# Feeding a state-space scan: inputs in SBUF, four f32 row groups, and no stacking through DRAM

## The chip, the core and the metric

The kernel runs on one core of a Trainium2 chip. Its time is the device time of one execution in microseconds: 2395.61 us is the median of three runs (2390.84 to 2396.46). Everything is computed in one launch.

## What is computed

One layer of a hybrid decoder on 304 token columns: 16 meta tokens, 256 prompt tokens and 8 x 4 sample tokens. Around the mixer stand two SwiGLU blocks; the change lies inside the mixer, in the S5 branch.

```python
z = rms(x) @ w_in                      # u_pool | u_ssm | gate a | gate b
a_out = pool_mix(u_pool)
# S5, 64 groups of 16 channels, 64 complex states each
lam_bar = exp(lam * exp(log_dt));  b_bar = (lam_bar - 1) / lam * b
bu = einsum('blgc,gpc->blgp', u, b_bar)
bu[:, 0] += lam_bar * h0               # each sequence starts from its own state
h[t] = lam_bar * h[t-1] + bu[t]
y = real(einsum('blgp,gcp->blgc', h, c)) + d * u
s = gelu(y);  s = s * sigmoid(s @ glu_w + glu_b)
x = x + (sig(gate_a) * (a_out @ w_a) + sig(gate_b) * (s @ w_b)) @ w_out
```

## The kernel before

Channels lie on partitions and tokens on columns, so a product with a weight matrix streams 304 columns (288 once the meta tokens are dropped). Each weight chunk (512 x 256, 512 KB) is split on the chip into a high part `whi` (ScalarE, L143) and a rest `wlo` (VectorE, L152); `mm3` (L241) makes three one-pass matmuls of each product. `proj` (L427) takes one chunk after another and calls `step` (L211) after each: the high part of a later chunk, the functions left by the last projection (`g.post`), the low part, the next load on SyncE's queue, and then pieces of a side program, `g.rate` pieces per step on average. A fraction is carried over, and `g.owed` may start below zero, which delays the side program by `LAG` steps. Three raw buffers and four of each part bound how far the loads run ahead.

In the mixer the side program is first the pool branch, and from the second `u_ssm` projection on the scan (`Scan.run`, L900). Its order is written out in `run`: for each of 16 blocks of 2 x 128 states twelve pieces (`rows`, L863), which are mostly one VectorE instruction each. The recurrence is turned into a real one by multiplying with tables of cosines and sines `ee`, which the setup (a side program in FFN 1) has computed and left in DRAM. Two `tensor_tensor_scan` instructions (L867) per block run along the 2 x 304 columns with the decay `d0`, which is zero where a sequence starts.

The scan's inputs are made as follows. `u_in` (L1026) multiplies the projection by the norm's factor, splits u into a high and a low part, writes u to DRAM on SyncE's queue (`usc`), and writes high, low and high again to DRAM on GpSimd's queue in the layout `stk[4, 96, 304]`. `load` (L816) fetches for each block 96 rows of that into one of two SBUF tiles, whose last 32 rows are ones at the columns where a sample sequence starts (`isc`), then `bl`, the matrices of the block, `ee`, and every second time u. `into` (L829) makes one one-pass matmul of 128 rows for each of three kinds (real, imaginary, sum) and two halves; ScalarE copies each result to a tile `bu`. The matrix holds the high part of the input map twice, its rest once, and the start states in its last rows, so that the start states enter in the same product.

`outof` (L838) multiplies the states by the output map `clhs`: for each of eight channel tiles twelve f32 matmuls with 32 columns of weights, which write four groups of 32 rows of one bank. `act` (L849) adds d * u and applies GELU.

PSUM has eight banks of 512 f32: four for projections, three (`psaux`) for small products, one (`pslong`) for the output group and for part of the down projections.

Of the kernel before, what the change touches and what calls it, by code (L numbers as in the profile page):

```python
# [18 lines left out]
P = 128  # L19
# [6 lines left out]
NB = 8  # L26
# [10 lines left out]
MIXRATE = 2.35  # L37
# [10 lines left out]
LAG = 7  # L48
BUFS = 6
KUFS = 8  # L50
# [6 lines left out]
def host_consts():  # L57
    import numpy as np

    c = np.zeros((P, NT + NTV + 2), np.float32)  # L60
    c[:, :NT] = 1.0
    c[:, 0] = 0.0
    c[:, S0:NT:NS] = 0.0
    c[:, NT:NT + 16] = np.arange(16)
    c[:, NT + 16:NT + NTV] = 16 * np.arange(NA)
    par = (np.arange(P) // 16) % 2
    c[:, NT + NTV] = par == 0
    c[:, NT + NTV + 1] = par == 1
    s = np.zeros((32, NT), np.float32)
    for b in range(NB):  # L70
        s[b, S0 + b * NS] = s[NB + b, S0 + b * NS] = 1.0
    return {"consts": c, "starts": s}
# [90 lines left out]
def setup(ctx, tc, I):  # L163
# [21 lines left out]
    g.isc = g.dram.tile([32, JB, NT], F32R, name="isc")  # L185
# [352 lines left out]
def ssm_setup(g):  # L538
# [6 lines left out]
    g.clhs = [C.tile([P, NJ, 32], F32, name=f"clhs{i}") for i in range(3)]  # L545
    g.esc = [g.dram.tile([P, 3, JB, NT], F32, name=f"esc{b}") for b in range(NJ // JB)]
    g.bsc = [g.dram.tile([P, 3 * JB, P], F32R, name=f"bsc{b}") for b in range(NJ // JB)]
    tv = g.hc[:, NT:NT + NTV]

    with ExitStack() as cs_:  # L550
# [163 lines left out]
        ah = [T(f"ah{i}", [P, NB, NJ]) for i in range(3)]  # L714
# [7 lines left out]
        tt(ah[2], ah[0], ah[1], ALU.add)  # L722
# [18 lines left out]
        ind = T("q1", [32, NT])  # L741
        nc.gpsimd.dma_start(ind, I["starts"])
        yield 1
        cx = [T(f"cx{i}", [P, 8, 2, 64]) for i in range(3)]
        for i in range(3):
            for a in range(2):
                ts_(cx[i][:, :, a], cs[i], g.hc[:, NT + NTV + a:NT + NTV + a + 1], None, ALU.mult)
                yield 1

        G = 4  # L750
        bds = {}

        def spread(h, i):
            if i == 0:
                bds[h] = T("bd", [P, G, 3, P], bufs=2)
                nc.gpsimd.memset(bds[h], 0.0)  # L756
            hj = slice(h * G, (h + 1) * G)
            bv = bds[h][:, :, i, :96].rearrange("p j (r a c) -> p j r a c", r=3, a=2)
            for a in range(2):
                for r in range(3):  # L760
                    nc.scalar.copy(bv[a * 64:(a + 1) * 64, :, r, a], bx[i][a * 64:(a + 1) * 64, hj])
            for r in range(2):
                nc.scalar.copy(bds[h][:, :, i, 96 + r * NB:96 + (r + 1) * NB], ah[i][:, :, hj].rearrange("p b j -> p j b"))

        def turned(h, q, jj, bl):
            ps = bank(g, "bt", aux=True)
            for i in range(3):
                nc.tensor.transpose(ps[:, i * P:(i + 1) * P], bds[h][:, q * JB + jj, i], g.ident)
# [4 lines left out]
        indr = sp.tile([32, JB, NT], F32R, name="indr")  # L773
        for h in range(NJ // G + 1):
            if h == NJ // G:
                for jj in range(JB):
                    nc.vector.tensor_copy(indr[:, jj], ind)
                nc.gpsimd.dma_start(g.isc, indr)
                yield 1
            if h < NJ // G:  # L780
                for i in range(3):
                    spread(h, i)
                    yield 1
            if h >= 1:
                for q in range(G // JB):
                    bl = sp.tile([P, 3 * JB, P], F32R, name=nm(g, "bl"), tag="bl", bufs=2)
                    for jj in range(JB):
                        turned(h - 1, q, jj, bl)
                        yield 1
                    nc.gpsimd.dma_start(g.bsc[(h - 1) * (G // JB) + q], bl)  # L790
        for i in range(3):
            for q in range(2):
                ps = bank(g, "ct", aux=True)
                for ii in range(4):
                    nc.tensor.transpose(ps[:, ii * P:(ii + 1) * P], cx[i][:, q * 4 + ii].rearrange("p a s -> p (a s)"), g.ident)
                nc.scalar.activation(g.clhs[i][:, q * 16:(q + 1) * 16].rearrange("p j c -> p (j c)"), ps,
                                     AF.Copy, scale=-1.0 if i == 1 else 1.0)
                yield 1


class Scan:


    def __init__(self, g, sp, usc, stk):
        self.g, self.sp, self.usc, self.up = g, sp, usc, stk
        self.st = g.mix.tile([P, 2, NB + 1, NJ], F32, name="states")
        self.stk = [sp.tile([P, JB, NT], F32R, name=f"stk{i}") for i in range(2)]
        for t in self.stk:
            g.nc.gpsimd.dma_start(t[96:], g.isc)
        self.sparts = []  # L810
        self.yps = {}
# [3 lines left out]

    def load(self, sb):  # L816
        g, sp, nc = self.g, self.sp, self.g.nc
        i, half = divmod(sb, 4 // JB)
        ee = sp.tile([P, 3, JB, NT], F32, tag="ee", name=nm(g, "ee"), bufs=2)
        bl = sp.tile([P, 3 * JB, P], F32R, tag="bl", name=nm(g, "bl"), bufs=1)  # L820
        nc.gpsimd.dma_start(self.stk[sb % 2][:96], self.up[i][half * JB:(half + 1) * JB].rearrange("j r t -> r j t"))
# [508 lines left out]
```

## Time and profile before

| | |
|---|---|
| median of three runs | 2395.61 us |
| profiled execution | 2394.65 us |
| its span, first to last instruction | 2392.9 us |
| TensorE busy | 2351.8 us, 98% |
| VectorE busy | 1592.3 us, 67% |
| ScalarE busy | 1013.1 us, 42% |
| GpSimd busy | 137.9 us, 6% |
| DMA | 443.27 MB, 185 GB/s |

Shares are means over the span; what an edit is worth is read in the stretch where it lies. PE is TensorE's matmuls, PEld its weight loads, DVE is VectorE, ACT ScalarE, POOL GpSimd, SP SyncE; an engine's name with a q is its queue. Matmuls overlap, and the duration of one is longer than the distance to the next, so distances between starts or counts per stretch are used for what one costs. An f32 matmul is two records, a one-pass matmul is one.

### The profile page before, as it was taken

Reading aid. Unit: us, or ns where it says so; the run is one execution under the profiler, and the core shown is the slowest. Engines: PE = TensorE matmul, PEld = TensorE weight load, DVE = VectorE, ACT = ScalarE, POOL = GpSimd, SP = SyncE. Lnnn points to the kernel's source line nnn. Section 1 sums busy time; section 2 is a strip of 40 time slices with the busy share of each in tenths; the row PEclk is TensorE's granted clock in tenths of the full one; section 3 lists DMA queues with packets and bytes.
Section 4 is the critical chain, followed back from the end, with each engine's and each line's share of the span. In section 5 each row is a group of like instructions: output and inputs, shape, how many; then the busy total and the mean of one; then the engine's idle time right before and its main releaser. Section 6 shows DMA issues by size and latency. Waiting matters only on the chain.

```text
span 2392.9 us, 42570 instructions
## 1 busy us (share of the span) xinstructions
PE 2351.8 (98%) x17321; PEld 2333.2 (98%) x17321; DVE 1592.3 (67%) x2416; ACT 1013.1 (42%) x1617; POOL 137.9 (6%) x233
## 2 busy tenths in 40 slices
PE   8999999999999999979999999999999999999998
PEld 7999999999999999979989999999999999999997
DVE  6788777776555557659889875555555555555555
ACT  5333333343564335434545544443333333333334
POOL 1000000001010002220101031000000000000000
PEclk9999999999999999989999999999999999999999
DMA  6555666666556446697778676455555555555553
GB/s 187 159 159 187 192 199 205 206 197 184 180 175 191 154 156 196 183 256 230 241 232 251 197 253 206 151 177 167 164 163 168 167 168 166 166 163 167 168 167 111
DMA packets 407076, 443.27 MB, mean 185 GB/s; under 512 B 25036, under 2 KB 393904, under 8 KB 406872
## 3 DMA queue, kind: packets, MB, share of 16 engines
q1 hardware_dynamic: 376512, 376.75, 50.5%
q0 software_dynamic: 30368, 63.80, 9.1%
q8 instruction: 136, 2.23, 0.4%
q14 instruction: 60, 0.49, 0.1%
HBM read 404.30 MB, written 36.51 MB: 184 GB/s over the span
## 4 chain that ended last, share of the span: by engine, by line
PE 81%; issue 7%; DVE 5%; DMA 5%; ACT 2%; POOL 1%; ACTq 0%; SPq 0%; DVEq 0%; POOLq 0%
PE pj L243 20%; PE pj L244 19%; PE pj L245 19%; PE dn L243 7%; PE dn L245 7%; PE dn L244 7%; DMA raw<-in_w_in 2%; DVE wlo L152 2%; ACT whi L143 1%; DMA raw<-in_w_branch_a 1%; DMA bl<-bsc 1%; DMA raw<-in_ffn_w_gate 1%; DVE bu L867 0%; POOL bd L756 0%; PE tx L415 0%
## 5 line engine op out<-in xcount | busy, mean ns | idle before, releaser
L152 DVE TENSOR_TENSOR wlo<-raw,whi 128x1024 fp32r<-128x1024 f32 x698 | 852.6, 1223 | 592.2 <-ACT whi L143 587.0
L143 ACT CAST whi<-raw 128x1024 fp32r<-128x1024 f32 x698 | 732.5, 1051 | 1116.9 <-PE pj L244 611.3
L243 PE MATMUL pj<-X,whi 128*128 128x304 f32 (+1 forms) x2432 | 739.1, 304 | 0.0
L244 PE MATMUL pj<-X,whi 128*128 128x304 f32 (+1 forms) x2432 | 733.1, 301 | 0.0
L245 PE MATMUL pj<-X,wlo 128*128 128x304 f32 (+1 forms) x2432 | 732.0, 301 | 0.0
L243 PE MATMUL pj<-Y,whi 128*128 128x288 f32 x1728 | 509.8, 295 | 0.7 <-DVE Y L272 0.7
L244 PE MATMUL pj<-Y,whi 128*128 128x288 f32 x1728 | 510.1, 295 | 0.0
L245 PE MATMUL pj<-Y,wlo 128*128 128x288 f32 x1728 | 508.7, 294 | 0.0
L243 PEld LDWEIGHTS pj<-X,whi 128*128 128x128 f32 x2432 | 459.6, 189 | 3.5 <-issue 2.8
L244 PEld LDWEIGHTS pj<-X,whi 128*128 128x128 f32 x2432 | 460.8, 189 | 0.0
L245 PEld LDWEIGHTS pj<-X,wlo 128*128 128x128 f32 x2432 | 460.4, 189 | 0.0
L243 PEld LDWEIGHTS pj<-Y,whi 128*128 128x128 f32 x1728 | 325.3, 188 | 1.4 <-DVE Y L272 0.9
L244 PEld LDWEIGHTS pj<-Y,whi 128*128 128x128 f32 x1728 | 324.8, 188 | 0.0
L245 PEld LDWEIGHTS pj<-Y,wlo 128*128 128x128 f32 x1728 | 324.7, 188 | 0.0
L243 PE MATMUL dn<-H,whi 128*128 128x304 f32 x704 | 213.6, 303 | 0.2 <-DVE x L481 0.2
L245 PE MATMUL dn<-H,wlo 128*128 128x304 f32 x704 | 213.0, 303 | 0.0
L244 PE MATMUL dn<-H,whi 128*128 128x304 f32 x704 | 212.2, 301 | 0.0
L244 PE MATMUL dn<-X,whi 128*128 128x288 f32 x704 | 207.9, 295 | 0.0
L243 PE MATMUL dn<-X,whi 128*128 128x288 f32 x704 | 207.8, 295 | 0.0
L245 PE MATMUL dn<-X,wlo 128*128 128x288 f32 x704 | 207.6, 295 | 0.0
L243 PEld LDWEIGHTS dn<-H,whi 128*128 128x128 f32 x704 | 132.3, 188 | 0.5 <-DVE x L481 0.5
L243 PEld LDWEIGHTS dn<-X,whi 128*128 128x128 f32 x704 | 132.7, 188 | 0.0
(274 smaller groups left out, 1981.7 us busy)
## 6 DMA issues: line engine op xcount, KB each, us to landing
raw<-in_ffn_w_gate SPq DMA_DIRECT2D x176, 512.0 KB, 3.6
raw<-in_ffn_w_up SPq DMA_DIRECT2D x176, 512.0 KB, 3.6
raw<-in_ffn_w_down SPq DMA_DIRECT2D x176, 512.0 KB, 3.5
raw<-in_w_in SPq DMA_DIRECT2D x96, 512.0 KB, 5.2
raw<-in_w_out SPq DMA_DIRECT2D x32, 512.0 KB, 4.2
esc<-ee POOLq DMA_DIRECT2D x16, 912.0 KB, 5.0
ee<-esc POOLq DMA_DIRECT2D x16, 912.0 KB, 8.0
raw<-in_w_branch_a SPq DMA_DIRECT2D x16, 512.0 KB, 4.7
```

What stands on the lines that cost most here:

```text
L143: self.g.nc.scalar.copy(hi, self.raw[i])
L152: self.g.nc.vector.tensor_tensor(lo, raw, hi.bitcast(F32), ALU.subtract)
L243: mm(ps, wh, x[0], start=start, stop=False)
L244: mm(ps, wh, x[1], start=False, stop=False)
L245: mm(ps, wl, x[0], start=False, stop=stop)
```

## The change

The stacked tiles, the copies of u in DRAM and the row of ones go. `Scan.input` keeps u of each of eight channel tiles in SBUF as f32. For one tile and one kind `into` makes four f32 matmuls of 32 rows each, from partitions 0, 32, 64 and 96 of u and of the matrices, into four banks: three of `psaux` and `pslong`. Four copies on ScalarE bring them to the tiles of both blocks of the channel tile. The start states are no longer in the product: `begun` adds them on VectorE, two small additions per block. The setup makes one matrix tile `bc` per channel tile, input and output map together, and `matrices` loads it. The scan runs in place (`k3` and `k2`), all rows come from one ring of 15 tiles, the first loads are issued after the second pool projection, and the side program's rate is 2.25 instead of 2.35 with a lag of 2 instead of 7.

```diff
-MIXRATE = 2.35
+MIXRATE = 2.25
-LAG = 7
-BUFS = 6
-KUFS = 8
+LAG = 2
+ROWS = 15
...
-    g.clhs = [C.tile([P, NJ, 32], F32, name=f"clhs{i}") for i in range(3)]
+    g.ah = C.tile([P, 2, NB, NJ], F32, name="ah")
...
-    g.bsc = [g.dram.tile([P, 3 * JB, P], F32R, name=f"bsc{b}") for b in range(NJ // JB)]
+    g.bsc = [g.dram.tile([P, 2, 3, P], F32, name=f"bsc{i}") for i in range(KW)]
...
-            b3 = bl[:, jj * 3:jj * 3 + 3].rearrange("p i s -> p (i s)")
-            nc.scalar.copy(b3, ps[:, :3 * P])
-            tt(b3[64:96 + NB], ps[64:96 + NB, :3 * P], b3[64:96 + NB].bitcast(F32), ALU.subtract)
+            nc.scalar.copy(bc[:, half].rearrange("p i s -> p (i s)"), ps[:, :3 * P])
...
+    def input(self, ps, r):
+
+        u = self.sp.tile([P, NT], F32, name=nm(self.g, "u"))
+        self.g.nc.vector.tensor_tensor(u, ps, r, ALU.mult)
+        self.u.append(u)
+
     def load(self, sb):
...
-        nc.gpsimd.dma_start(self.stk[sb % 2][:96], self.up[i][half * JB:(half + 1) * JB].rearrange("j r t -> r j t"))
-        nc.gpsimd.dma_start(bl, g.bsc[sb])
-        nc.gpsimd.dma_start(ee, g.esc[sb])
...
+        g.nc.gpsimd.dma_start(ee, g.esc[sb])
+        return dict(ee=ee, bu={})
+
+    def matrices(self, i):
+        g = self.g
+        self.mats[i] = self.sp.tile([P, 2, 3, P], F32, tag="bc", name=nm(g, "bc"), bufs=2)
+        g.nc.gpsimd.dma_start(self.mats[i], g.bsc[i])
+
+    def into(self, i, pair, ri):
+
+        g = self.g
+        pss = []
+        for q in range(4):
+            rows = slice(q * 32, (q + 1) * 32)
+            ps = bank(g, "bu", aux=True, pool=g.pslong if q == 3 else None)[:, :NT]
+            g.nc.tensor.matmul(ps, self.mats[i][rows, 0, ri], self.u[i][rows], start=True, stop=True)
+            pss.append(ps)
+        for s in pair:
+            s["bu"][ri] = self.tile("row", ROWS)
+        for q, ps in enumerate(pss):
+            g.nc.scalar.copy(pair[q // JB]["bu"][ri][:, q % JB], ps)
...
+        def begun(k, ri):
+            tt(k[:, :, S0::NS], k[:, :, S0::NS], g.ah[:, ri, :, js].rearrange("p b j -> p j b"), ALU.add)
...
-                lambda: tt(k3, k1, k3, ALU.subtract),
-                lambda: scan(gr, d0, k3),
+                lambda: turned(k3, k1, k3, 0),
+                lambda: scan(k3, d0, k3),
...
+    def first(self):
+
+        self.matrices(0)
+        self.nxt = self.load(0)
+
     def run(self):
...
+        pair = [self.nxt, self.load(1)]
+        for ri in (2, 1, 0):
+            self.into(0, pair, ri)
+            yield 1
+        done, acts = None, None
+        for i in range(KW):
+            nxt = [dict(bu={}) for _ in range(half)]
+            for h in range(half):
+                sb = i * half + h
+                rows = self.rows(sb, pair[h])
+                if sb >= 1 and sb + 1 < nb:
+                    new = self.load(sb + 1)
+                    (nxt[0] if h else pair[1])["ee"] = new["ee"]
+                for n, row in enumerate(rows):
+                    row()
+                    if h == 0 and n == 3 and done is not None:
+                        self.outof(i - 1, done)
+                        acts = self.act(i - 1)
+                    if h == 0 and n == 8 and i + 1 < KW:
+                        self.matrices(i + 1)
+                    if h and i + 1 < KW and n in (4, 7, 10):
+                        self.into(i + 1, nxt, {4: 2, 7: 1, 10: 0}[n])
+                    yield 1
...
-    def u_in(i, ps):
-        u = Z()
-        nc.vector.tensor_tensor(u, ps, norm.r, ALU.mult)
-        hi, lo = uparts[i % 2]
-        nc.scalar.copy(hi, u)
-        nc.vector.tensor_tensor(lo, u, hi.bitcast(F32), ALU.subtract)
-        uk = g.dram.tile([P, NL], F32, name=nm(g, "usc"))
-        nc.sync.dma_start(uk, u[:, NMETA:])
-        stk = g.dram.tile([4, 96, NT], F32R, name=nm(g, "stk"))
-        for k, x in enumerate((hi, lo, hi)):
-            nc.gpsimd.dma_start(stk[:, k * 32:(k + 1) * 32], x)
...
+                if p == 1:
+                    scan.first()
...
+                g.post += [lambda q=q: scan.input(q, norm.r) for q in ps]
```

On TensorE, at the scan's first products, before: two `bu` products behind the ninth weight chunk after the first u projection, three behind the tenth, one behind the eleventh; `pj` are the matmuls of the projection.

```order
L245 MATMUL pj_11573<-X_10133,wlo_11501 128x304
L835 MATMUL bu_11625<-stk_10586,bl_11566 128x304
L835 MATMUL bu_11628<-stk_10586,bl_11566 128x304
L243 MATMUL pj_11572<-X_10180,whi_11529 128x304
...
L245 MATMUL pj_11573<-X_10232,wlo_11531 128x304
L835 MATMUL bu_11662<-stk_10586,bl_11566 128x304
L835 MATMUL bu_11665<-stk_10586,bl_11566 128x304
L835 MATMUL bu_11669<-stk_10586,bl_11566 128x304
...
L245 MATMUL pj_11573<-X_10330,wlo_11561 128x304
L835 MATMUL bu_11702<-stk_10586,bl_11566 128x304
```

The scan's first products on TensorE now, behind the third weight chunk after the first u projection: each four `bu` are one kind, one for each row group.

```order
L240 MATMUL pj_10937<-X_9989,wlo_10924 128x304
L812 MATMUL bu_11034<-u_10964,bc_10441 128x304
L812 MATMUL bu_11036<-u_10964,bc_10441 128x304
L812 MATMUL bu_11038<-u_10964,bc_10441 128x304
L812 MATMUL bu_11040<-u_10964,bc_10441 128x304
L812 MATMUL bu_11048<-u_10964,bc_10441 128x304
L812 MATMUL bu_11050<-u_10964,bc_10441 128x304
L812 MATMUL bu_11052<-u_10964,bc_10441 128x304
L812 MATMUL bu_11054<-u_10964,bc_10441 128x304
L238 MATMUL pj_10936<-X_10035,whi_10962 128x304
```

The first products moved six chunks, 144 projection matmuls, up in TensorE's order, and two groups of four stand back to back.

On GpSimd's queue, before, at the start of the scan: twelve writes of the stacks of four tiles, and behind them the scan's first loads.

```order
L1036 DMA stk_11457<-Y_10597 4x32x304
L1036 DMA stk_11467<-Y_10599 4x32x304
L1036 DMA stk_11467<-Y_10600 4x32x304
L1036 DMA stk_11467<-Y_10599 4x32x304
L821 DMA stk_10586<-stk_11315 96x2x304
L822 DMA bl_11566<-bsc_715 128x768
L823 DMA ee_11565<-esc_699 128x1824
L826 DMA u_11570<-usc_11313 128x288
```

The same queue now: the first matrices and tables stand among the pool branch's small transfers, two projections further up.

```order
L1010 DMA out<-up_10399 8x4x256
L803 DMA bc_10441<-bsc_712 128x768
L797 DMA ee_10443<-esc_696 128x1824
L960 DMA hist_10445<-in_state_pool 120x256
...
L1010 DMA out<-up_10888 8x4x256
L797 DMA ee_11032<-esc_697 128x1824
L803 DMA bc_11249<-bsc_713 128x768
L797 DMA ee_11327<-esc_698 128x1824
```

What the queue carries for a channel tile is now two `ee` and one `bc`; the stack writes, the stack reads, the second `bl` and u are gone.

On VectorE, one block of the scan now (before, the same rows without L864, and with the scans' results in other tiles):

```order
L872 TENSOR_TENSOR row_11110<-row_11109,row_11110 128x608
L864 TENSOR_TENSOR row_11110<-row_11110,ah 128x2x8
L849 SCALAR_TENSOR_TENSOR row_11110<-d_1665_11106,row_11110 128x608
L879 TENSOR_TENSOR row_11111<-row_11100,ee_10443 128x608
L872 TENSOR_TENSOR row_11111<-row_11109,row_11111 128x608
L864 TENSOR_TENSOR row_11111<-row_11111,ah 128x2x8
L849 SCALAR_TENSOR_TENSOR row_11111<-d_1665_11106,row_11111 128x608
```

Between each difference and its scan stands one addition of 2 x 8 columns more.

## Rows read from the trace of the kernel before

**Rows 1.** Page, engine totals: busy us, share of the span, instructions.

```profile
PE 2351.8 (98%) x17321; PEld 2333.2 (98%) x17321; DVE 1592.3 (67%) x2416; ACT 1013.1 (42%) x1617; POOL 137.9 (6%) x233
```

**Rows 2.** Stretches: from:to, length, busy us (instructions) by engine, clock, DMA share.

```profile
960.00:1020.00 60.00, 60.00 (x432) 59.96 (x432) 38.71 (x77) 22.93 (x38) 14.32 (x23) 1.00 0.65 176
...
1020.00:1080.00 60.00, 45.74 (x301) 45.06 (x301) 35.72 (x49) 25.78 (x45) 13.64 (x21) 0.86 0.98 259
...
1600.00:1800.00 200.00, 200.00 (x1514) 200.00 (x1513) 110.98 (x148) 74.72 (x87) 0.00 (x0) 1.00 0.53 166
```

**Rows 3.** The same table, stretches of 10 us.

```profile
1020.00:1030.00 10.00, 4.19 (x30) 3.94 (x29) 0.03 (x1) 1.04 (x1) 0.54 (x1) 0.83 1.15 286
1030.00:1040.00 10.00, 6.00 (x24) 6.04 (x25) 5.28 (x7) 3.61 (x6) 4.80 (x7) 0.50 0.86 227
```

**Rows 4.** Timeline: start, us, engine, line, what, count [idle before <- releaser].

```profile
1028.89 1.04 ACT L143 CAST whi<-raw 128x1024 fp32r<-128x1024 f32 x1 [12.78 <-DMA raw<-in_w_in]
...
1033.99 0.59 PE L835 MATMUL bu<-stk,bl 128*128 128x304 f32 x1 [9.80 <-DMA bl<-bsc]
```

**Rows 5.** DMA issues, 1017 to 1345 us: count, KB each, median us to landing.

```profile
raw<-in_w_in SPq DMA_DIRECT2D x65, 512.0 KB, 5.8
...
ee<-esc POOLq DMA_DIRECT2D x16, 912.0 KB, 8.0
...
bl<-bsc POOLq DMA_DIRECT2D x16, 384.0 KB, 4.4
...
stk<-stk POOLq DMA_DIRECT2D x16, 228.0 KB, 9.0
...
stk<-Y POOLq DMA_DIRECT2D x12, 152.0 KB, 10.2
```

**Rows 6.** Timeline, first matmul of the stage behind the scan.

```profile
1355.62 0.29 PE L243 MATMUL pj<-Y,whi 128*128 128x288 f32 x1
```

**Rows 7.** Lines, 1017 to 1345 us: count | busy us, mean ns | idle before.

```profile
L152 DVE TENSOR_TENSOR wlo<-raw,whi 128x1024 fp32r<-128x1024 f32 x84 | 102.4, 1219 | 41.6 <-ACT whi L143 41.3
...
L867 DVE TENSOR_TENSOR_SCAN bu<-d,kk 128x608 f32<-128x608 f32 x32 | 45.5, 1422 | 0.7
...
L836 ACT COPY bu<-bu 128x304 f32<-128x304 f32 x96 | 35.8, 411 | 31.7 <-PE bu L835 31.7
...
L889 DVE TENSOR_TENSOR kk<-kk,kk 128x608 f32<-128x608 f32 x16 | 12.6, 790 | 0.3
...
L1042 DVE TENSOR_TENSOR z<-pj,rs_y 128x288 f32<-128x288 f32 x28 | 11.4, 449 | 0.0
...
L895 DVE TENSOR_TENSOR kk<-bu,ee 128x576 f32<-128x576 f32 x15 | 11.3, 751 | 0.0
...
L835 PE MATMUL bu<-stk,bl 128*128 128x304 f32 x96 | 25.1, 325 | 17.5 <-DMA bl<-bsc 9.8 <-ACT bu L836 7.7
...
L884 DVE TENSOR_TENSOR states<-kk,kk 128x18 f32<-128x18 f32 x30 | 4.4, 192 | 0.4
...
L853 DVE SCALAR_TENSOR_TENSOR gy<-u,vec,yps 128x288 f32<-128x288 f32 x7 | 3.5, 500 | 0.0
```

**Rows 8.** Chain that ended last: start us, us, what.

```profile
1053.94 8.56 DMA raw<-in_w_branch_a
```

**Rows 9.** Timeline of TensorE around one output group.

```profile
1247.44 0.30 PE L244 MATMUL pj<-X,whi 128*128 128x288 f32 x1
1247.57 0.29 PE L245 MATMUL pj<-X,wlo 128*128 128x288 f32 x1
1247.79 1.66 PE L846 MATMUL yps<-kk,clhs 128*32 128x288 f32 x24
1249.39 0.40 PE L243 MATMUL pj<-X,whi 128*128 128x288 f32 x1
1249.62 0.29 PE L244 MATMUL pj<-X,whi 128*128 128x288 f32 x1
```

**Rows 10.** Timeline, f32 matmuls with two columns each.

```profile
940.28 0.72 PE L343 MATMUL ss<-ones,acc 128*128 128x2 f32 x6
```

More of the change, by code (lines that the diff above doesn't have):

```diff
@@ L68, in host_consts @@
     c[:, NT + NTV + 1] = par == 1
[L69 to L72, printed above, removed]
+    return {"consts": c}
 class Ctx:
@@ L713, in ssm_setup @@
         t8 = T("q1", [P, NB, NJ])
-        ah = [T(f"ah{i}", [P, NB, NJ]) for i in range(3)]
+        ah = [g.ah[:, i] for i in range(2)]
         tt(ah[0], h0[0], bc(lbr), ALU.mult)
@@ L721, in ssm_setup @@
         tt(ah[1], ah[1], t8, ALU.add)
-        tt(ah[2], ah[0], ah[1], ALU.add)
         yield 1
@@ L765, in turned, with spread @@
-        def turned(h, q, jj, bl):
+        bds = [T(f"bd{k}", [P, 3, 4, 2, 16]) for k in range(2)]
+        for bd in bds:
+            nc.gpsimd.memset(bd, 0.0)
+            yield 1
+        def spread(m):
+            for i in range(3):
+                for a in range(2):
+                    rows = slice(a * 64, (a + 1) * 64)
+                    nc.scalar.copy(bds[m % 2][rows, i, :, a], bx[i][rows, m * 4:(m + 1) * 4])
+        def turned(bc, half, src):
             ps = bank(g, "bt", aux=True)
@@ L791, in ssm_setup @@
[L791 to L798, printed above, removed]
+                nc.tensor.transpose(ps[:, i * P:(i + 1) * P], src(i), g.ident)
@@ L801, with __init__ @@
 class Scan:
-    def __init__(self, g, sp, usc, stk):
-        self.g, self.sp, self.usc, self.up = g, sp, usc, stk
+    def __init__(self, g, sp):
+        self.g, self.sp = g, sp
         self.st = g.mix.tile([P, 2, NB + 1, NJ], F32, name="states")
-        self.stk = [sp.tile([P, JB, NT], F32R, name=f"stk{i}") for i in range(2)]
-        for t in self.stk:
-            g.nc.gpsimd.dma_start(t[96:], g.isc)
+        self.u = []
         self.sparts = []
-        self.yps = {}
+        self.mats, self.yps = {}, {}
@@ L876, in rows @@
             nc.scalar.activation(d0[:, jj], g.hc[:, :NT], AF.Copy, scale=g.rdec[:, j:j + 1])
-        k1, k3, k2 = (self.tile("kk", KUFS) for _ in range(3))
+        k1, k3, k2 = (self.tile("row", ROWS) for _ in range(3))
         s["k"] = (k1, k2, k3)
-        gr, gi = bi, br
         js = slice(sb * JB, (sb + 1) * JB)
+        def begun(k, ri):
+            tt(k[:, :, S0::NS], k[:, :, S0::NS], g.ah[:, ri, :, js].rearrange("p b j -> p j b"), ALU.add)
         def states():
@@ L898, in rows @@
+                lambda: tt(L(k1), L(k1), L(er), ALU.mult),
                 states]
+    def first(self):
+        self.matrices(0)
+        self.nxt = self.load(0)
     def run(self):
+        half = 4 // JB
         nb = NJ // JB
-        nxt = self.load(0)
-        yield 1
-        yield 1
-        for k in range(6):
-            self.into(0, nxt, k)
-            yield 1
-        pair, acts = [], None
-        for sb in range(nb):
-            cur = nxt
-            rows = self.rows(sb, cur)
-            nxt = self.load(sb + 1) if sb + 1 < nb else None
-            for n, row in enumerate(rows):
-                row()
-                if nxt is not None and 6 <= n < 12:
-                    self.into(sb + 1, nxt, n - 6)
-                if len(pair) == 4 // JB and n == 3:
-                    i = (sb - 1) // (4 // JB)
-                    self.outof(i, pair)
-                    acts = self.act(i, pair[0]["u"])
-                    pair = []
-                yield 1
-                if acts is not None and n >= 6 and next(acts, None) is None:
-                    acts = None
-            pair.append(cur)
@@ L926, in run @@
-        self.outof(KW - 1, pair)
-        yield 1
-        yield from self.act(KW - 1, pair[0]["u"])
+        pair = [self.nxt, self.load(1)]
+        for ri in (2, 1, 0):
+            self.into(0, pair, ri)
+            yield 1
+        done, acts = None, None
[16 more added lines that the diff above has]
+                        self.into(i + 1, nxt, {4: 2, 7: 1, 10: 0}[n])
+                    yield 1
+                    if acts is not None and n >= 6 and next(acts, None) is None:
+                        acts = None
+            done, pair = pair, nxt
@@ L930, in store @@
+        self.outof(KW - 1, done)
+        yield 1
+        yield from self.act(KW - 1)
     def store(self, O, sp):
@@ L1049, in mixer @@
             sp = cs.enter_context(g.tc.tile_pool(name="scan", bufs=1))
-            scan = Scan(g, sp, usc, stks)
+            scan = Scan(g, sp)
             pool = Pool(g, O)
-            uparts = [(part(g, "Y", NT), part(g, "Y", NT)) for _ in range(2)]
             dparts, aparts = [], []
```

90 lines of the change are left out of this document (27 added, 63 removed).

## Prediction

> **What bounds the kernel now.** I read the page's engine totals first: TensorE is busy for 98% of the span [rows 1], so an edit can only pay where TensorE stands idle, runs slowly, or gets more or less to do. Next I read the table of stretches. At full pace TensorE issues 432 matmuls of 304 columns in 60 us, 0.139 us each, and of 288 columns 1514 in 200 us, 0.132 us each [rows 2]. The stretch from 1020 to 1080 us has only 301, and its granted clock is 0.86 [rows 2]. That is the start of the scan, which the change rewrites. The finer table shows 30 matmuls from 1020 to 1030 us and 24 from 1030 to 1040, at a granted clock of 0.83 and 0.50 [rows 3].
>
> The timeline says why. TensorE waits 9.80 us, until 1033.99, for the scan's first matrices `bl` to land, and ScalarE waits 12.78 us for a weight chunk at the same time [rows 4]. The DMA share is 1.15 from 1020 to 1030 [rows 3]. What is in flight there is the stacking: `stk<-Y` takes 10.2 us to land, `stk<-stk` 9.0 us, for 152 and 228 KB, while a 512 KB weight chunk takes 5.8 us [rows 5]. After its idle time TensorE runs at the lower of its two clocks (1.2 of 2.4 GHz: the 0.50 of rows 3) before it is back at full speed.
>
> After that VectorE sets the pace. I count in steps, one per weight chunk of 24 matmuls: 12 in what is left of the u projections, 2 for pool_w, 48 for the gate with branch A, 32 for the second gate, 94 in all. The wait that ends at 1033.99 lies behind step 9, and the next stage's first matmul stands at 1355.62 [rows 6], so 85 steps take 321.6 us, 3.78 each. VectorE's work per step, from [rows 7]: one wlo, 1.22; 2.35 scan rows. A block of 12 rows is five full-width ones like L889 at 0.79, two scans at 1.42, four like L895 at 0.75 and two small ones of 0.19, which is 10.2, or 0.85 per row; 2.35 of them are 2.00. Gates (two products of 0.45 per projection, L1042, and two for branch A per 6 steps) 0.30, GELU (four operations of about 0.47, like L853, once in 24 rows) 0.18. Sum 3.70. TensorE's per step: 24 x 0.132 = 3.18, six `bu` in 5.1 steps 0.16, and the output group (1.78 us, below) once in 10.2 steps, 0.17: 3.51. VectorE is behind by 0.19 in each. The chain shows the partner of that: a late wlo frees its raw buffer late, and the next load then takes 8.56 us [rows 8].
>
> **The change part by part.**
>
> *Stacking gone.* The 24 `stk<-Y` (three for each of eight tiles), 16 `stk<-stk` and the copies of u through DRAM go, and the first matrices and the first table block are loaded a whole projection stage earlier. What TensorE would wait for at its first group is then u alone, one product on VectorE of about 0.47 us that is issued two steps ahead. So the 9.8 us go, and with them the slow clock: from 1034 to 1040 TensorE did 24 matmuls where 43 fit, 19 x 0.139 = 2.6 us. Together -12.4. What could be late there next is a weight chunk; ScalarE's 12.78 us came from the same crowd of transfers and should go with it.
>
> *Four row groups.* 96 one-pass matmuls become 24 groups of four f32 matmuls with 32 rows each. The trace has no row group, but the output product is its sibling in columns: four column groups, f32. There 12 matmuls are 24 records, and these run from 1247.79 to 1249.39: six rounds of four, 0.265 each. Had the four not run side by side, it would be four times that. The slot before is 0.22 instead of 0.13, the one behind 0.23 instead of 0.13 [rows 9]: 0.19 for going in and out, 1.78 in all. For 304 columns a group of four is two rounds of 0.28 plus 0.19: 0.75, and I take 0.8. Before, four `bu` cost 4 x 0.139 = 0.56, so 24 groups add 5.8 us of TensorE time. Bounds: 0.56 a group (nothing added), and 4 x 0.56 + 0.19 = 2.4 us a group if the four run one behind the other (44 us added). Weight loads lie between: TensorE's three f32 matmuls with two columns each make six loads of 128 columns in 0.72 us, 0.12 each [rows 10]. Eight of them in a row, and the last round behind, give 0.96 + 0.28 + 0.19 = 1.4 a group.
>
> *Where these 5.8 us lie.* In the gate stages TensorE's step becomes 3.18 + 0.17 + 3 x 0.8 per 10.7 steps, 0.22, = 3.57, still under VectorE. There it is covered. Without that cover it would be 0.06 a step, 4 us. Not covered: the first three groups, 2.4 - 0.8 = 1.6, in steps 3 and 4. The second group stands right behind the first and needs the same four banks, so it waits for ScalarE's four copies (35.8/96 = 0.37 each [rows 7]): 1.5 and the way there and back, 1.9.
>
> *VectorE.* In place or not, the row operations have the same sizes. New are two small additions per block where the states enter; the nearest row is L884 with 0.19, so 0.03 per row. A step is 1.22 + 2.25 x 0.88 + 0.48 = 3.68, against 3.70: no change of pace. Steps 4 to 9 had no scan and ran at TensorE's 24 x 0.139 = 3.34; with it VectorE needs 1.22 + 1.98 + 0.24 (two products for u per four steps) = 3.44: 6 x 0.1 = +0.6. What goes (two casts and differences per projection, outside the scan) lies beside TensorE in steps that were not late. The scan starts at step 3 instead of 8 and lasts 199 pieces / 2.25 = 88 steps, so it ends near step 90; the last 4 or 5 steps run at TensorE's own 3.2: 4.5 x 0.4 = -1.8.
>
> *Loads.* On GpSimd's queue `bc` now waits for the output group (the buffer it replaces is read there), and the next `ee` is queued behind it. It is issued 8 rows, 3.5 steps or 13 us, ahead of its use; a load of that size (`bl`) lands in 4.4 us [rows 5], so nobody waits. Fewer bytes in flight should shorten the 8.56 us loads; from 0 to -4.5 (what 321.6 has over 85 x 3.70 and the 2.6), I take -1. Bank waits at the second and third group of each tile, one or two steps apart: 0 to +4, I take 0.
>
> *Setup.* The matrices are built with fewer copies inside FFN 1, where TensorE issues without a gap. Nothing.
>
> Sum: -12.4 + 1.6 + 1.9 + 0.6 - 1.8 - 1 = -11.1. The profiled execution took 2394.65 us, 1.75 of it around the span, and is 1 us under the median of 2395.61. 2394.65 - 11.1 gives 2384.
>
> **The rivals.** *Weight loads one behind the other*: 1.4 a group. TensorE's step is then 3.18 + 0.17 + 0.39 = 3.74, over VectorE's by 0.06; over the 74 steps with 288 columns and scan 4.5 us, and 0.6 for each of the four groups before them, 2.4: +7, which gives 2391, no change. For it: a full load in rows 10 is as dear as 0.12 even behind idle streams. Against: in the output product the loads of four column groups did not show up beside the rounds, but they have 32 columns and not 128. The Trainium skill's page "TensorE: Matmul & The Clock Gate", section "LDWEIGHTS (loading the stationary operand)", states that a load takes by its columns, and a load of 32 rows as long as one of 128. No run here has a load of 32 rows; by that rule this rival is the likelier the less loads of different row groups overlap.
>
> *The four run one behind the other*: 2.4 a group. TensorE's step is 3.18 + 0.17 + 0.67 = 4.02; 0.34 over VectorE's for 74 steps is 25, and the four groups before them cost 1.6 more each, 6: -11 + 31 = +20, or 2415, slower. TensorE takes over from VectorE at 1.2 us a group, and the gain is used up near 1.6. Against it stands that column groups do overlap [rows 9]; for it, that f32 is two records a matmul, which in issue order could block each other, and that nothing in the trace uses row groups.
>
> *The load waits go too*: VectorE's chain no longer stretches, all of the 4.5 us: 2380, and 2377 if the bank wait of 1.9 and half of the 1.6 do not show either.
>
> *The stall only moves*: the first group is reached 20 us earlier, while `ee` loads 912 KB and weights run on; a weight chunk is late there and half of the 12.4 stays: 2390.
>
> **How the numbers follow.** Forecast with four at once 0.60 (own range 2377 to 2391), load waits gone 0.08, stall moved 0.08, loads in a row 0.14, one behind the other 0.10. Runs of this kernel differ by up to 0.24%, so 0.3%, 7.2 us, is what can be told from no change: faster means under 2388.4, slower over 2402.8. Faster: 0.60 x 0.83 + 0.08 + 0.02 = 0.60. Slower: 0.10 + 0.14 x 0.25 + 0.03 = 0.17, and same the 0.23 left. The range leaves out about 0.1 on either side: 2374 to 2404.
>
> **What would show it.** Right: no wait over 2 us from 1000 to 1040 us, granted clock 1.00 throughout that stretch; the input groups last near 0.8 us each as two rounds of four; VectorE over 9.0 in ten through the gate stages; the glu projection starts 8 to 13 us earlier. Wrong: groups of 1.4 or 2.4 us, TensorE's waits for `row` copies by ScalarE over 8 us in all, `bc` or `u` as a releaser of TensorE, or a pace in the gate stages other than 3.68 to 3.78 us a step.

## The result, and the profile after

The change makes the kernel faster: 2366.81 us, the median of four runs (2366.51 to 2366.92), against 2394.65 for the kernel before (four runs, 2390.84 to 2396.46). The ratio on record is 0.9874, 95% interval 0.9859 to 0.9889; the two medians alone give 0.9884. The forecast was 2384 with a range of 2374 to 2404. The direction is right and the gain far too small, 27.8 us where 11.1 stood, and the time lies 7 us under the range.

The engine totals of the kernel after, against [rows 1]:

```profile
PE 2344.9 (99%) x17345; PEld 2316.0 (98%) x17345; DVE 1578.7 (67%) x2405; ACT 980.1 (41%) x1443; POOL 85.1 (4%) x159
```

TensorE was already busy for 98%, so the totals hardly show 28 us. The stretches do, against [rows 2, 3] (columns as there):

```profile
960.00:1020.00 60.00, 59.52 (x427) 57.74 (x426) 42.87 (x79) 25.63 (x46) 3.79 (x7) 1.00 0.58 180
1020.00:1080.00 60.00, 58.43 (x453) 53.66 (x452) 53.57 (x79) 29.98 (x55) 2.12 (x4) 1.00 0.60 190
...
1020.00:1030.00 10.00, 10.00 (x75) 9.41 (x74) 8.91 (x13) 4.32 (x9) 0.53 (x1) 1.00 0.74 250
1030.00:1040.00 10.00, 10.00 (x79) 8.85 (x79) 8.61 (x14) 5.18 (x11) 0.53 (x1) 1.00 0.46 146
```

From 1020 to 1080 us TensorE issues 453 matmul records where there were 301 (an f32 matmul counts twice), and the granted clock is 1.00 where it was 0.86. The hole at the scan's start is gone. But that is not all of the 27.8. TensorE's timeline gives the points that divide the program (start, us, engine, line, what, count, idle before):

```profile
931.13 0.72 PE L338 MATMUL ss<-ones,acc 128*128 128x2 f32 x6
...
994.80 0.79 PE L812 MATMUL bu<-u,bc 32*128 32x304 f32 x8
996.08 1.72 PE L812 MATMUL bu<-u,bc 32*128 32x304 f32 x8 [0.48 <-ACT row L817]
...
1054.46 0.40 PE L238 MATMUL pj<-Y,whi 128*128 128x288 f32 x1 [1.57 <-DVE Y L267]
...
1326.52 0.29 PE L238 MATMUL pj<-Y,whi 128*128 128x288 f32 x1
```

These are the mixer's first sums (940.28 before [rows 10]), the scan's first two groups, the first matmul of branch A and the first of the glu projection (1355.62 before [rows 6]). The third point stood before at:

```profile
1074.22 0.40 PE L243 MATMUL pj<-Y,whi 128*128 128x288 f32 x1 [0.65 <-DVE Y L272]
```

The differences of these starts, in us, with the forecast's terms put into the same parts:

| part | before | after | change | forecast |
|---|---|---|---|---|
| up to the mixer's first sums (FFN 1, setup beside it) | 940.28 | 931.13 | -9.15 | 0 |
| from there to branch A (u, pool, the scan's start) | 133.94 | 123.33 | -10.61 | -12.4 + 1.6 + 1.9 + 0.6 = -8.3 |
| gate stages, 76 chunks | 281.40 | 272.06 | -9.34 | -1.8 - 1 = -2.8 |
| from the glu projection to the end | 1037.28 | 1038.48 | +1.20 | 0 |
| span | 2392.9 | 2365.0 | -27.9 | -11.1 |

The part that the prediction spent most words on was nearly right. Two parts in which it expected little or nothing carry the miss: 9 us ahead of the mixer, and 6.5 more than forecast in the gate stages. Of the first, 1.3 us is the start of the kernel, where a transpose waits for its input (11.99 us before, 10.72 after) in a line that the change does not touch. The +1.20 behind the glu projection was not looked into: this part takes 1038.4 to 1038.8 us in all profiles of kernels built on after, and 1037.3 to 1037.5 in those built on before.

In the gate stages a step is now 272.06 / 76 = 3.58 us; it was 281.40 / 76 = 3.70. The lines of this stretch, against [rows 7] (1017 to 1325 us):

```profile
L148 DVE TENSOR_TENSOR wlo<-raw,whi 128x1024 fp32r<-128x1024 f32 x86 | 105.0, 1220 | 15.8 <-ACT whi L139 15.5
...
L139 ACT CAST whi<-raw 128x1024 fp32r<-128x1024 f32 x85 | 89.4, 1054 | 58.9 <-PE pj L239 29.6 <-DMA raw<-in_w_in 14.7 <-DMA raw<-in_w_branch_a 9.2
L817 ACT COPY row<-bu 128x304 f32<-128x304 f32 x84 | 28.5, 425 | 29.0 <-PE bu L812 29.0
L812 PE MATMUL bu<-u,bc 32*128 32x304 f32 x168 | 16.7, 466 | 0.0
...
L864 DVE TENSOR_TENSOR row<-row,ah 128x16 f32<-128x16 f32 x30 | 5.7, 192 | 1.0
```

Three numbers matter. TensorE waits 0.0 us ahead of the scan's input products, where L835 waited 17.5 (the first groups, with their 0.48, lie ahead of this stretch). VectorE stands idle 15.8 us ahead of wlo, where it stood 41.6. And 168 records, 21 groups of four, keep TensorE busy 16.7 us: 0.80 a group.

The transfers of that stretch, against [rows 5] (count, KB each, median us to landing):

```profile
raw<-in_w_in SPq DMA_DIRECT2D x63, 512.0 KB, 4.1
ee<-esc POOLq DMA_DIRECT2D x14, 912.0 KB, 6.7
...
bc<-bsc POOLq DMA_DIRECT2D x6, 384.0 KB, 4.6
```

A weight chunk of 512 KB lands in 4.1 us, where it took 5.8.

### The profile page after: what moved, and what is told of

The parts are those of the page before. It is cut to its first block, busy times and chain, and to the rows that moved or that the text cites. A ratio compares the mean times of both kernels' runs of the same rounds, so it can differ in the third digit from the quotient of the medians.

```text
span 2365.0 us, 42243 instructions
## 1 busy us (share of the span) xinstructions
PE 2344.9 (99%) x17345; PEld 2316.0 (98%) x17345; DVE 1578.7 (67%) x2405; ACT 980.1 (41%) x1443; POOL 85.1 (4%) x159
## 4 chain that ended last, share of the span: by engine, by line
PE 98%; DVE 1%; ACT 0%; DMA 0%; SPq 0%; issue 0%; ACTq 0%; DVEq 0%
PE pj L238 24%; PE pj L239 24%; PE pj L240 24%; PE dn L238 8%; PE dn L240 8%; PE dn L239 8%; PE bu L812 1%; PE yps L828 0%; PE tx L410 0%; PE bt L758 0%; DMA tok<-in_x_sample 0%; DVE wlo L148 0%; DVE acc L327 0%; ACT y L1183 0%; PE ty L1145 0%
## 5 line engine op out<-in xcount | busy, mean ns | idle before, releaser
L238 PEld LDWEIGHTS pj<-X,whi 128*128 128x128 f32 x2432 | 457.7, 188 | 11.1 <-issue 10.1
L238 PEld LDWEIGHTS dn<-X,whi 128*128 128x128 f32 x704 | 132.6, 188 | 0.0
L239 PEld LDWEIGHTS dn<-X,whi 128*128 128x128 f32 x704 | 132.4, 188 | 0.0
```

The costliest lines, as they stand in the source:

```text
L238: mm(ps, wh, x[0], start=start, stop=False)
L239: mm(ps, wh, x[1], start=False, stop=False)
```

## The experiments

Except for the three that start from the kernel before, each is the kernel after with something of before put back, and every one computes the full result. A price with a plus sign is the difference of medians to 2366.81. Every run in 1 to 8 took longer than the slowest of after (2366.92), but with 4 to 12 runs each, which spread by 1.3 to 10 us, the sizes are uncertain by 1 to 3 us; this matters for the small ones. The parts come from one profiled execution of each kernel, and it is said where that lies far from the median.

**1. The setup's transposes.** The kernel before turns 120 squares in the setup; the one after 48. TensorE's groups in FFN 1, before:

```profile
L768 PE MATMUL bt<-ident,bd 128*128 128x128 f32 x96 | 15.0, 272 | 0.0
L795 PE MATMUL ct<-ident,cx 128*128 128x128 f32 x24 | 3.4, 272 | 0.0
```

and after:

```profile
L758 PE MATMUL bt<-ident,cx 128*128 128x128 f32 x24 | 3.9, 272 | 0.0
L758 PE MATMUL bt<-ident,bd 128*128 128x128 f32 x24 | 3.9, 271 | 0.0
```

The run puts 72 more into the setup, with results that nobody reads:

```diff
             turned(bc, 1, ...)
             yield 1
+            for _ in range(3):
+                ps = bank(g, "xt", aux=True)
+                for i in range(3):
+                    nc.tensor.transpose(ps[:, i * P:(i + 1) * P], cx[i][:, m]..., g.ident)
+                yield 1
```

> The changed kernel with 72 more 128x128 transposes in the setup inside FFN 1, in 24 sets of three, as many as the change took away. Theory S (the setup's transposes stand in TensorE's queue and TensorE never waits there, so each costs its full time): the start of the mixer moves back by 7 to 9 us, total 2374 to 2376. Theory of the forecast (setup costs nothing): 2367.

Measured: 2375.25 us (ratio to before 0.9916, 0.9903 to 0.9930), +8.4, or 0.117 us a transpose. In the profiled execution, 1.4 us under the median, the mixer's first sums start at 938.24 instead of 931.13, and both later parts are unchanged to 0.02 us (123.33 and 272.04):

```profile
938.24 0.72 PE L338 MATMUL ss<-ones,acc 128*128 128x2 f32 x6
```

This is 7.1 us, 0.10 a transpose. With the 1.3 us of the kernel's start it is nearly the whole of the first part: TensorE has no gap there (0.0 us of idle time ahead of the transposes), and what is taken off its queue is time.

**2. VectorE's load.** Sixteen additions of 576 columns, one per block of the scan, on VectorE alone:

```diff
-                lambda: tt(k3, bi, ed, ALU.mult),
+                lambda: (tt(k3, bi, ed, ALU.mult), tt(L(bs), L(er), L(es), ALU.add)),
```

> The changed kernel with one more VectorE addition of 2 x 288 columns per block (16 of 0.75 us, 12 us in all, 0.14 us a step); its result is not used. Theory V (VectorE's step is 3.68 us, over TensorE's 3.57, and is the pace): +10 to +12 us, 2377 to 2379. Theory L (VectorE's instructions overlap at their ends, a wlo costs 1.14 and not 1.22, so a step is about 3.45 us and has 0.1 us left): 0 to +4 us, 2367 to 2371.

Measured: 2369.02 (0.9890, 0.9877 to 0.9904), +2.2 for 12 us of VectorE's work; the gate stages take 273.51. VectorE does not set the pace of the kernel after.

**3. The side program's rate.**

```diff
-MIXRATE = 2.25
-LAG = 2
+MIXRATE = 2.35
+LAG = 7
```

> The changed kernel with the side program's old pace (rate 2.35, lag 7). The changed kernel took 2366.81 us. Theory L (the gate stages were slow before because weight chunks came late behind the stack, matrix and u transfers; the pace of the scan did not matter): the scan still ends in time (199 pieces / 2.35 + 7 = 92 of 94 steps), so 2365 to 2370. Theory V (the forecast's: VectorE sets the pace, and the rate and early start decide how far it falls behind): some 8 us come back, 2373 to 2378.

Measured: 2369.41 (0.9895, 0.9881 to 0.9908), +2.6, of which 2.3 in the gate stages (274.39; from the sums to branch A 122.81).

**4 to 6. The transfers, with nobody waiting for them.** Run 4, the reads (stack-sized blocks, the other half of the matrices, u):

```diff
     def load(self, sb):
+        g.nc.gpsimd.dma_start(xs, g.esc[sb][:96, 0:JB, 0, :NL])
+        ... (half of bsc, or u-sized, per block)
         g.nc.gpsimd.dma_start(ee, g.esc[sb])
```

> The changed kernel with the old reads added per block, which nobody waits for: 96 x 2 x 288 f32 of stack size, half as much again of matrices (384 KB every second block), 144 KB of u every second block, from DRAM into unused SBUF. Theory L: loads of weight chunks land later again (median of the w_in loads back from 4.0 towards 5.8 us), ScalarE waits for raw chunks over 50 us in the scan's stretch instead of 28, and the time rises by 4 to 10 us to 2371 to 2377. Theory V: VectorE and TensorE have the same work, 2366 to 2368.

Measured: 2368.38 (0.9891, 0.9878 to 0.9905), +1.6, less than theory L has. Run 5, the writes, three of 152 KB behind each u as before:

```diff
         self.u.append(u)
+        xw = self.g.dram.tile([4, 96, NT], F32, name=nm(self.g, "xw"))
+        for k in range(3):
+            self.g.nc.gpsimd.dma_start(xw[:, k * 32:(k + 1) * 32], u)
```

> The changed kernel with the 24 stack writes of before added (each 128 x 304 f32 to DRAM as 4 x 32 rows), behind each u on GpSimd's queue; nobody reads them. Theory C (the writes by themselves hold up the weight chunks): ScalarE waits over 8 us for one chunk between 990 and 1050 us, TensorE stands idle for 3 to 10 us there, time +4 to +12 us over 2366.8. Theory Q (only what TensorE's first product needs is late): loads take longer, time +0 to +3 us.

Measured: 2374.84 (0.9911, 0.9896 to 0.9926), +8.0. Run 6, both together:

> The changed kernel with the stack writes and the block reads of before added, that is with nearly all of the transfers that went, but with nothing that waits for them. If transfers alone made before slow in this stage (theory C, L): 2375 to 2385. If it was what waits for them and the hand-over of the banks (theories Q, B): 2367 to 2372.

Measured: 2379.35 (0.9931, 0.9917 to 0.9944), +12.5. The profiled execution of this run is its slowest, 4.3 us over the median, so its parts are on the high side. Its stretches, in the columns of [rows 2], show the hole of [rows 3] again, though no instruction of TensorE, ScalarE or VectorE reads what was written:

```profile
1030.00:1040.00 10.00, 6.94 (x54) 6.12 (x52) 5.68 (x8) 1.05 (x1) 1.67 (x3) 1.00 1.01 314
1040.00:1050.00 10.00, 7.84 (x38) 7.03 (x39) 7.96 (x11) 6.33 (x13) 4.31 (x7) 0.66 0.71 184
1050.00:1060.00 10.00, 6.38 (x58) 5.07 (x57) 4.26 (x6) 1.48 (x2) 1.72 (x3) 0.90 1.00 326
```

ScalarE's timeline there says where it begins: it waits for three weight chunks, 5.54, 6.73 and 7.41 us.

```profile
1032.98 1.05 ACT L139 CAST whi<-raw 128x1024 fp32r<-128x1024 f32 x1 [5.54 <-DMA raw<-in_w_in]
1040.75 1.04 ACT L139 CAST whi<-raw 128x1024 fp32r<-128x1024 f32 x1 [6.73 <-DMA raw<-in_w_in]
1054.49 1.05 ACT L139 CAST whi<-raw 128x1024 fp32r<-128x1024 f32 x1 [7.41 <-DMA raw<-in_w_branch_a]
```

And TensorE's waits (us, times, longest) show how it reaches TensorE, under other names:

```profile
PE bu L824 <- ACT row L829: 5.7, 2, 5.2
...
PE pw L238 <- DVE z L1036: 3.6, 1, 3.6
PE pj L238 <- DVE z L1036: 2.3, 1, 2.3
```

ScalarE stands at its cast until the chunk has come, and behind the cast in its queue are the copies that free the banks and the functions that the next stage needs. From the sums to branch A the run takes 136.65 us (after 123.33, before 133.94), in the gate stages 275.77.

**7. Everything at once.** The edits of 1, 3, 4 and 5 together:

> The kernel after with four things of before put back at once, each of which was measured alone: the 72 transposes of the setup (+8.4 us), the writes of three copies of each u to DRAM on GpSimd's queue and the reads of stack size (+12.5 together), and the old rate and lag of the side program (2.35 and 7; +2.6). Nobody reads what the added transfers bring, and the results are the reference's. Theory A (the parts add up, because they lie in different stretches or are different waits): 2366.8 + 8.4 + 12.5 + 2.6 = 2390.3, between 2387 and 2393; then 2 to 7 us of the difference to before are left for what no kernel has put back. Theory O (the late weight chunks and the slower side program are the same wait, counted twice, and the sum is less): 2380 to 2386, and 8 to 15 us would be left without a cause. Theory M (a later start of the scan puts its rows into a stretch with more transfers, and the two make each other worse): over 2394.

Measured: 2391.55 (0.9986, 0.9976 to 0.9997), +24.7; the sum of the single prices is 2390.3. In total they add up; by parts they do so less well, for in the gate stages the rate costs 2.3 (run 3) and the transfers 3.7 (run 6), and both together here 3.3. And one wait for data is in this run already: TensorE waits 7.2 us for a `bc`, which shares GpSimd's queue with the added transfers.

**8. And a wait for the data.** As 7, with u of the first channel tile read back from DRAM when the scan begins:

```diff
+        self.g.nc.gpsimd.dma_start(self.u[0], self.xw[:, :32])
         pair = [self.nxt, self.load(1)]
```

> As the run before it, and the scan's first four groups of TensorE have to wait for the transfers: when the side program comes to the scan, u of the first channel tile is read back from DRAM (152 KB, behind the writes on GpSimd's queue) into its own place, with the same values. That is the wait for the stack, 9.8 us of TensorE's idle time before. Theory A: what is left to before (about 5 us) is this wait, which lies partly beside the weight chunks that are late at the same place: 2392 to 2397, a ratio to before of 0.999 to 1.001, and a TensorE wait of 4 to 10 us for u at the first groups. Rival C (the wait is covered by the late chunks, as when the first matrices were loaded early in the kernel before, which gave no gain): within 1.5 us of the run without it.

Measured: 2395.98 (0.9999, 0.9990 to 1.0008): 4.4 over run 7, and the time of before. TensorE's timeline:

```profile
1028.43 1.40 PE L831 MATMUL bu<-u,bc 32*128 32x304 f32 x8 [9.06 <-DMA u<-xw]
...
1069.29 1.40 PE L831 MATMUL bu<-u,bc 32*128 32x304 f32 x8 [8.42 <-DMA bc<-bsc]
```

A wait of 9.06 us costs 4.4 in the medians, while the part to branch A grows by 7.7 us from the one profile to the other. That other waits (7.2 us for `bc` and 2.5 for bank copies in run 7) lie beside it in part is likely, but not shown.

The parts of these runs, in the columns of the table above (us, profiled execution of each):

| run | to the sums | to branch A | gate stages |
|---|---|---|---|
| before | 940.28 | 133.94 | 281.40 |
| after | 931.13 | 123.33 | 272.06 |
| 5, writes | 929.96 | 132.19 | 272.04 |
| 6, writes and reads | 930.64 | 136.65 | 275.77 |
| 7, all | 939.38 | 134.67 | 275.39 |
| 8, all and the wait | 938.82 | 142.33 | 275.35 |

The profiled executions of runs 7 and 8 are 1.6 us under and 1.1 over their medians. The total of run 8 meets before, but its parts do not: it has 8.4 us more ahead of branch A and 6.0 less in the gate stages. That the totals meet is so far a coincidence, and these 6.0 us of before are in none of the edits.

**9 to 11. Taking single waits out of the kernel before.** A fourth bank for the products (`pslong` for the fourth of six):

```diff
-        ps = bank(self.g, "bu", aux=True)[:, :NT]
+        ps = bank(self.g, "bu", aux=True, pool=self.g.pslong if k == 3 else None)[:, :NT]
```

> The kernel before with a fourth bank for its one-pass products: the fourth of each six goes to pslong. In the trace of before all 7.7 us in which TensorE stands idle from 1080 to 1345 us are waits for a `bu` bank that ScalarE still has to copy. Theory B (the hand-over of three banks ties TensorE to ScalarE, which is itself held by late weight chunks): these waits fall below 3 us and the time by 4 to 7 us from before. Theory L2 (the late weight chunks are the cause; with more banks TensorE waits for the chunk instead): the sum of TensorE's waits stays within 2 us, so does the time.

Measured: 2393.16 against 2395.94 (0.9989, 0.9978 to 1.0001). The waits for ScalarE's copies (7.7 us before) are gone, and others have come:

```profile
PE bu L835 <- DMA bl<-bsc: 9.4, 1, 9.4
PE bu L835 <- DVE gy L853: 6.3, 4, 2.5
PE pw L243 <- DVE z L1042: 6.2, 1, 6.2
```

The first matrices and tables loaded early, as the change does, with the stacks left:

```diff
-        nc.gpsimd.dma_start(bl, g.bsc[sb])
-        nc.gpsimd.dma_start(ee, g.esc[sb])
+        if sb:
+            nc.gpsimd.dma_start(bl, g.bsc[sb])
+            nc.gpsimd.dma_start(ee, g.esc[sb])
```

(the first pair is issued when the scan object is made)

> The kernel before with the first `bl` and `ee` loaded where the scan's tiles are made, ahead of all stack writes on GpSimd's queue. Theory Q (TensorE waits 9.8 us because `bl` stands behind twelve stack writes on its queue): the wait falls under 3 us, the slow clock goes, and the time falls by 8 to 12 us. Theory C (the crowd of stack writes is the cause: the first stack read, which TensorE needs too, and the weight chunk land as late as `bl` did): the wait stays over 6 us with the stack or a weight chunk as releaser, time within 4 us of before.

Measured: 2394.16 (0.9999, 0.9985 to 1.0013). TensorE now waits for the stack instead of `bl`, 6.6 us in the profiled execution, which is 5.8 us under the median of its runs:

```profile
PE bu L844 <- DMA stk<-stk: 6.6, 1, 6.6
PE bu L844 <- ACT bu L845: 6.4, 8, 1.9
```

The six products in three pairs, so that three banks suffice:

```diff
-                if nxt is not None and 6 <= n < 12:
-                    self.into(sb + 1, nxt, n - 6)
+                if nxt is not None and n in (6, 8, 11):
+                    for k in ((0, 1), (2, 3), (4, 5))[(6, 8, 11).index(n)]:
+                        self.into(sb + 1, nxt, k)
```

> The kernel before, with the six products that make the next block's inputs issued as three pairs, with rows 6, 8 and 11 of the running block, instead of one with each of the rows 6 to 11: no weight chunk is followed by more than two of them, so three banks suffice wherever ScalarE copies within a step. All transfers and results are as before. It is about the part of the gate stages (281.4 us from the first matmul of branch A to that of the glu projection) that the kernel after with all old transfers, rate and transposes does not give back (275.4). Theory B (the three banks cost this part: products too close for ScalarE's copies): TensorE's 7.7 us of waits for the copies fall below 3 and the gate stages take 275 to 278 us; time 3 to 6 us under before. Rival L (ScalarE is late because of late weight chunks, and TensorE waits whatever the spacing): the waits stay above 5 us or turn into others, gate stages 280 to 283, time within 2 us of before.

Measured: 2396.22 (1.0002, 0.9992 to 1.0012). The waits stay:

```profile
PE bu L835 <- DMA bl<-bsc: 9.1, 2, 8.6
PE pw L243 <- DVE z L1043: 7.1, 1, 7.1
PE bu L835 <- ACT bu L836: 6.4, 7, 2.5
```

In the profiled execution, 4.0 us under the median, the gate stages take 276.6 us, as theory B had it, with the waits that rival L had, so the parts do not decide; the time is L's. The gate stages take 278.35, 279.24 and 276.59 us in runs 9, 10 and 11, and the part to branch A 135.72, 129.53 and 137.38. So what runs 9 and 11 save in the gate stages of their profiles, 3.0 and 4.8 us, they lose in part ahead of branch A, 1.8 and 3.4. None of the three takes anything off that could be told from no change: in these traces one wait goes and TensorE waits for the next thing that is late.

## Why the prediction was right in part and wrong in two steps

Two steps failed. The prediction put the change of the setup at nothing, and run 1 measured 8.4 us for it. And it took VectorE for the engine that sets the pace of the gate stages, so that the pace could not change; 12 us more on VectorE cost 2.2 us (run 2), and these stages became 9.3 us shorter where 2.8 were forecast. Of these 9.3, put-back rate and transfers account for 3.3 (run 7), and the cause of the other 6.0 stays open.

*Setup: failed.* The prediction said: "The matrices are built with fewer copies inside FFN 1, where TensorE issues without a gap. Nothing." The second half of that sentence speaks against the "Nothing" behind it. It looked at ScalarE's copies and left out that the same functions issue transposes on the one engine that has no gap. Priced from rows of before, 72 of them at 15.0 / 96 = 0.16 us would have given -11; run 1 measured 8.4 (7.1 in its profile).

*The pace of the gate stages: failed.* "After that VectorE sets the pace", and with the change "3.68, against 3.70: no change of pace." A step is 3.58, outside the 3.68 to 3.78 that the prediction had set itself as a sign, and it is the number which it had worked out for TensorE itself (3.57; 24 x 0.132 is 3.17 and not 3.18 there) and called covered. That VectorE's sum of 3.70 met the pace of before was luck: in the trace of before no wait of TensorE is for wlo, and in the gate stages TensorE is busy for 273.7 of 281.4 us, 3.60 a step. VectorE's sum was made of listed durations, and these are longer than the instruction's place in the queue. VectorE's timeline after:

```profile
1007.29 0.79 DVE L872 TENSOR_TENSOR row<-row,row 128x608 f32<-128x608 f32 x1
1008.11 0.19 DVE L864 TENSOR_TENSOR row<-row,ah 128x16 f32<-128x16 f32 x1
1008.22 1.23 DVE L148 TENSOR_TENSOR wlo<-raw,whi 128x1024 fp32r<-128x1024 f32 x1
1009.37 1.42 DVE L849 TENSOR_TENSOR_SCAN row<-d,row 128x608 f32<-128x608 f32 x1
1010.70 0.77 DVE L879 TENSOR_TENSOR row<-row,ee 128x608 f32<-128x608 f32 x1
```

From wlo's start to the next it is 1.15 us, not 1.23, and from the scan's 1.33, not 1.42. The Trainium skill's page "Perfetto Trace Analysis", section "Optimizing Scalar/DVE Operations", says the same: a part of a profiled duration, the acknowledgement of the write, lies beside the next instruction. The trace agrees: 0.08 and 0.09 us lie beside it here. And one of the rows quoted spoke against the step: VectorE idled 41.6 us ahead of wlo for ScalarE's whi [rows 7], which an engine that sets the pace does not do. Run 2 settles it for the kernel after; no run puts work on VectorE in the kernel before.

*Loads: the mechanism was named, its size was off.* "Fewer bytes in flight should shorten the 8.56 us loads; from 0 to -4.5 (...), I take -1." Landing fell from 5.8 to 4.1 us. Late chunks reach TensorE through bank copies and through the inputs of the next matmuls (run 6), and the transfers alone, without anyone waiting for them, cost 12.5 us (run 6), most of it ahead of the gate stages. Of the gate stages' gain, run 7 gives back 3.3; the other 6.0 are open. Where they lie can be read. From 1080 to 1345 us TensorE stands idle for 7.7 us before and not at all in run 7, with as much traffic (columns as in [rows 2]; before, then run 7):

```profile
1080.00:1345.00 265.00, 257.29 (x1970) 246.67 (x1969) 240.38 (x325) 130.75 (x228) 25.27 (x44) 0.99 0.77 237
1080.00:1345.00 265.00, 265.00 (x2092) 246.02 (x2091) 248.32 (x357) 130.69 (x224) 28.31 (x50) 1.00 0.77 240
```

The 7.7 us are the waits for bank copies in [rows 7]. Runs 9 and 11 changed banks and order in the kernel before and did not turn them into time. Nor does run 7 bring back all of the late chunks: in the gate stages ScalarE waits 57.4 us for chunks before, 30.2 in run 7 and 23.9 after. One rival no run has tested: before, the write of each u to DRAM stands on SyncE's queue among the weight loads, and holds it until u is made (SPq is that queue, L1033 the write):

```profile
SPq L1033 <- DVE z L1028: 7.8, 6, 1.9
```

*The stall at the scan's start: nearly right in size, half right in mechanism.* Forecast for this part -8.3, measured -10.61; no wait over 0.5 us is left at the first groups and the clock is 1.00. But the price of 12.4 was laid on TensorE's wait for `bl`. Loading `bl` early is worth nothing by itself (run 10), and the transfers lengthen this part with no such wait, by 8.9 us in run 5 and 13.3 in the longest execution of run 6. One more wait of TensorE went that the prediction does not have, ahead of pool_w, and it is back in run 6 with 3.6 us; before:

```profile
PE pw L243 <- DVE z L1042: 3.8, 1, 3.8
```

So that the size was met is partly luck. The crowd of transfers, which the prediction named as the reason, was the cost through the weight chunks as much as through the scan's own data.

*Row groups: right.* Forecast 0.8 us a group, measured 0.80 as busy time and 0.82 as a place in the queue (0.95 between the starts of the matmuls on either side, less 0.13 for one of them). The rival by which weight loads of 32 rows would queue one behind the other (1.4) fell. The rule cited beside it, that a load takes by its columns, did not bind, and the trace agrees with it: loads of 32 rows are listed at 183 ns, those of 128 rows at 189. The same page of the Trainium skill, "TensorE: Matmul & The Clock Gate", section "The mechanism", says that loads for other row groups are pulled ahead of running matmuls. The 0.82 us a group agrees with that. The bank wait of the second group was 1.3 instead of 1.9: 0.48 ahead of its first matmul, and 0.8 within it, for it takes 1.65 us from its start to the next matmul.

*Scan in place, the small additions, the earlier loads:* 0.19 us forecast and listed for an addition (0.11 from its start to the next); TensorE does not wait for `bc`. VectorE is busy for 0.92 of the gate stages, as forecast, but the glu projection starts 29.1 us earlier, not 8 to 13.

*The rivals.* Nearest came the one in which the load waits go too (2380, or 2377 without bank waits), still 10 us too slow: that load waits go is right, but that they stretch VectorE's chain is not, and its bound of 4.5 us was taken from VectorE's wrong pace. The stall did not move, and the four row groups ran neither one behind the other nor with their loads in a row.

## What to carry to other kernels

Before an edit is called free, list every instruction it adds or removes by engine, and price those on the saturated engine first: here even setup work cost its place in the queue. A pace made of summed durations should be tested against the idle time in the same rows, and against what the saturated engine itself waits for. Traffic through DRAM was paid here by the loads beside it, so price what a transfer delays, and don't expect a gain from removing the wait that happens to be named.

## What was not expected of the hardware

- 24 writes of 152 KB on GpSimd's queue, which nobody waits for, cost 8.0 us through 512 KB loads on SyncE's queue (run 5); 16 stack-sized reads with their companions cost 1.6 (run 4), and together 12.5. That this is more than the sum of 9.6 is not certain at a spread of 5 to 6 us in each.
- The granted clock fell to 0.66 in run 6 (1040 to 1050 us) behind 3 us of idle time in the 10 us ahead; so the idle time was paid twice there.
- 128 x 128 transposes listed at 272 ns cost 0.10 (profile) to 0.12 us (medians) each in a full queue (run 1).
- A load of 32 rows and 128 columns of f32 weights is listed at 183 ns, one of 128 rows at 189, and yet four f32 matmuls on four row groups, with eight such loads, take 0.82 us.
